# Local attention: one 128x128 score matrix for both key blocks, transposed once, spread apart before the product with the values

## The chip, the cores and the metric

The kernel runs on one core of a Trainium2 chip. The metric is the device time of one execution in microseconds. The core's engines work side by side, each through its own queue in order: TensorE (PE; its weight loads are PEld), VectorE (DVE), ScalarE (ACT), GpSimd (POOL), and SyncE (SP), whose queue issues the DMAs here.

## The reference

One decoder layer: x (4096 x 1024, float32) is projected to eight attention heads, to a gated linear attention and to gates; both branches are gated, joined, projected and normalised. The change touches the sliding-window attention alone (8 query heads of 64 in two groups that share a key and value head each, blocks of 128 rows, window 128):

```python
kb, vb = with_prev(k), with_prev(v)          # this block's 128 keys and the 128 before it
scores = einsum('bnqhgd,bnkhd->bnhgqk', qb, kb) * 64 ** -0.5
dist = qi + BLOCK - ki                       # ki from 0 to 255
in_window = (dist >= 0) & (dist < WINDOW)
scores = where(in_window & has_prev, scores, -inf)
m = maximum(scores.max(-1), sink)
p = exp(scores - m)
probs = p / (p.sum(-1) + exp(sink - m))
out = einsum('bnhgqk,bnkhd->bnqhgd', probs, vb)
```

A query q sees key k of its own block if k <= q, and key k of the block before if k > q. So for each pair (q, k) in 128 x 128 exactly one of the two scores counts.

## The kernel before, in words

The sequence is cut into 32 blocks n of 128 rows, and the work into three stages, one after the other. Stage A does the attention branch for all blocks, stage B the linear attention, stage C the output projection and the normalisation. Matrices are split in a rounded high half and the rest (`split`, L97), so a projection (`project`, L130) is three matmuls for each of eight slices of the 1024 inputs: with high weights, low weights, and low inputs (L135, L136, L137). The engines' instruction orders are made by a scheduler from the order in which the program is written and from which buffers are free; a tile pool with `bufs=1` has one buffer per tag, so a new tile waits until the last reader of the one before is done.

Stage A, the loop over n at L397, projects block n (`pq` queries, `pkv` keys and values, `pg` the gate) and weaves in the softmax and the output of block n-1, written as generators: each `next` emits the next piece between two pieces of a projection.

- `a_scores` (L286): for each group g and pair h2 of heads, four matmuls (L306) write scores of two heads against 256 keys into one PSUM bank `psc`. For each head VectorE adds the mask, scales by 0.125, writes the result `s` to SBUF and reduces the maximum (L316). Then come small 4-wide operations for a group (L329, L330), ScalarE's exponential of 128x256 with its sum (L333), small ones again (L337, L338), and GpSimd's scaling of each head by the reciprocal `rec` (L341).
- `a_out` (L345): `turn(g, b)` transposes four heads' 128x128 blocks for key block b on TensorE (L355) and splits the result in `ph` (ScalarE) and `pl` (VectorE). `mul(g, b)` multiplies both with the values `vvs` into the bank `po` (L367, L368). ScalarE and VectorE add the two halves of `po` to `att` (L371, L372).
- Four more things share the engines in each block: the rotary work and copies of `a_q` and `a_kv`, the transposes `tk` (keys) and `tq` (queries) with their splits `kd` and `qs`, the gate `sg` with its transposes `tg`, and the load of x for the block after next, cast on GpSimd to `xh` (L102) and subtracted on VectorE to `xl` (L105).

PSUM has four tags with two banks each: `pj` (projections), `tp` (transposes), `c` (scores) and `d` (`po`).

Of the kernel before, what the change touches and what calls it, by code (L numbers as in the profile page):

```python
# [19 lines left out]
P = 128  # L20
# [6 lines left out]
NEG = -3.0e38  # L27
# [23 lines left out]
def layer_kernel(  # L51
# [35 lines left out]
    def bank(tag, name):  # L87
        return ps.tile([P, 512], F32, tag=tag, name=name)
# [49 lines left out]


    with ExitStack() as pa:  # L140
        wr = pa.enter_context(tc.tile_pool(name="wra", bufs=6))
        e1 = pa.enter_context(tc.tile_pool(name="e1", bufs=1))
        e2 = pa.enter_context(tc.tile_pool(name="e2", bufs=2))
        a1 = pa.enter_context(tc.tile_pool(name="a1", bufs=1))
        a2 = pa.enter_context(tc.tile_pool(name="a2", bufs=2))
        a4 = pa.enter_context(tc.tile_pool(name="a4", bufs=4))
        a12 = pa.enter_context(tc.tile_pool(name="a12", bufs=12))

        xs = [load_x(0, act, dve)]
        wq = load_group(wr, w_a, 0, 512, 0, 512, True)  # L150
# [73 lines left out]
        def swapped(n):  # L224
            return n % 4 < (n - 1) % 4
# [59 lines left out]

        def a_scores(n, qs):  # L286

            cur, prv = n % 4, (n - 1) % 4
            lo, hi = min(cur, prv), max(cur, prv)
            mask = msk[:, (2 if n == 0 else 1) if swapped(n) else 0]  # L290
# [4 lines left out]
            rec = a2.tile([P, 8], F32, tag="rec", name=f"rec{n}")  # L295
            pn = []
            for g in range(2):
                gs = slice(4 * g, 4 * g + 4)
                sc = []
                for h2 in range(2):  # L300
                    psc = bank("c", f"psc{n}_{g}_{h2}")
                    for e in range(2):
                        h = 4 * g + 2 * h2 + e
                        o = psc[:, e * 256 : (e + 1) * 256]
                        for hl in range(2):
                            pe.matmul(  # L306
                                o,
                                qs[:, h, :],
                                kd[:, g, hl, lo : hi + 1 : hi - lo, :],
                                start=(hl == 0),  # L310
                                stop=(hl == 1),
                            )
                    for e in range(2):
                        h = 4 * g + 2 * h2 + e
                        s = a12.tile([P, 256], F32, tag="s", name=f"s{n}_{h}")
                        dve.tensor_tensor_reduce(  # L316
                            out=s,
                            in0=psc[:, e * 256 : (e + 1) * 256],
                            in1=mask,
                            scale=0.125,  # L320
                            scalar=NEG,
                            op0=ALU.add,
                            op1=ALU.max,
                            accum_out=mx[:, h : h + 1],
                        )
                        sc.append(s)
                    if h2 == 0:
                        yield
                dve.scalar_tensor_tensor(ngm[:, gs], mx[:, gs], -1.0, nsnk[:, gs], ALU.mult, ALU.min)  # L329
                dve.tensor_tensor(es[:, gs], ngm[:, gs], snk[:, gs], ALU.add)  # L330
                for i in range(4):
# [7 lines left out]
                for i in range(4):  # L339
                    h = 4 * g + i  # L340
                    pool.tensor_scalar(sc[i], sc[i], rec[:, h : h + 1], 1.0, ALU.mult, ALU.mult)  # L341
                pn.append(sc)
                yield pn

        def a_out(n, pn, sg):  # L345
# [3 lines left out]
            pos_ = [bank("d", f"po{n}_{g}") for g in range(2)]  # L349
            parts = {}  # L350

            def turn(g, b):
                pt = bank("tp", f"pt{n}_{g}_{b}")
                for i in range(4):
                    pe.transpose(  # L355
                        pt[:, i * P : (i + 1) * P], pn[g][i][:, b * P : (b + 1) * P], ident
                    )
                ph = a2.tile([P, 512], F32R, tag="ph", name=f"ph{n}_{g}_{b}")
                pl = a2.tile([P, 512], F32R, tag="pl", name=f"pl{n}_{g}_{b}")
                split(ph, pl, pt, act, dve)  # L360
                parts[g, b] = ph, pl

            def mul(g, b):
                po = pos_[g]
                ph, pl = parts.pop((g, b))
                lh = vvs[n if (b == 0) == swapped(n) else n - 1][:, g, :]
                pe.matmul(po, lh, ph, start=(b == 0), stop=False)  # L367
                pe.matmul(po, lh, pl, start=False, stop=(b == 1))  # L368
                if b == 1:
                    m, c = (slice(0, 64), slice(64, 128)) if g == 0 else (slice(64, 128), slice(0, 64))  # L370
                    act.copy(tmp[m], po[c])  # L371
                    dve.tensor_tensor(att[m], po[m], tmp[m], ALU.add)  # L372

            turn(0, 0)
            turn(0, 1)
            yield
            mul(0, 0)
            turn(1, 0)
            yield
            mul(0, 1)  # L380
            turn(1, 1)
            yield
            mul(1, 0)
            yield
            mul(1, 1)
            yield
            tg = bank("tp", f"tg{n}")
            for j in range(4):
# [8 lines left out]
        for n in range(NB):  # L397
# [460 lines left out]
```

## Time and profile before

| | |
|---|---|
| three runs, median (lowest to highest) | 1752.09 us (1750.44 to 1753.18) |
| the profiled execution | 1752.42 us, its span 1750.6 us |
| TensorE matmul busy | 1716.2 us, 98% of the span |
| VectorE, ScalarE, GpSimd busy | 1094.8, 847.9, 456.6 us |
| granted TensorE clock, mean | 0.993 |

The span is what the profiler saw of the program; the execution's own time is 1.8 us longer. A matmul's row gives its own duration, with a modelled end, and matmuls overlap: what one costs TensorE is the distance from its start to the next start. The waits of a group tell what ended the idle time ahead of its instructions. Stage A takes up roughly the first 700 us, stage B the time up to some 1280, stage C the rest.

### The profile page before, as it was taken

The page shows a single profiled execution, that of the slowest core. Times are in us where ns is not written, and L with a number is a line of the kernel's source. Part 1 is how long each engine was busy: PE and PEld are TensorE (multiplying, and loading weights), DVE is VectorE, ACT ScalarE, POOL GpSimd, SP SyncE. Part 2 cuts the span into 40 slices and gives each one's busy share as a digit, 9 for nine tenths or more (in the row PEclk, how much of TensorE's full clock was granted, in tenths as well). Part 3 has the DMA queues.
Part 4 walks back from the last instruction along what each step waited for, and adds up shares of the span by engine and source line. Part 5 has one row for each costly group of instructions (what it writes and reads, how often), then busy time and mean ns, then how long its engine had stood idle before and what let it go on. Part 6 is the DMA issues. An engine that isn't in the chain of part 4 may idle for free.

```text
span 1750.6 us, 27011 instructions
## 1 busy us (share of the span) xinstructions
PE 1716.2 (98%) x9722; PEld 1474.6 (84%) x9722; DVE 1094.8 (63%) x2802; ACT 847.9 (48%) x2128; POOL 456.6 (26%) x633
## 2 busy tenths in 40 slices
PE   7999999999999998999999999999999899999998
PEld 6788888888888887888888888888888788888886
DVE  6766666666666677566665565565556755555555
ACT  5555555455555556555555555555555622222221
POOL 3222222222222244322222222222222412222221
PEclk9999999999999999999999999999999899999999
DMA  6211111111111123111111111111111444444442
GB/s 204 91 37 37 37 37 37 43 49 37 37 37 37 37 73 105 37 37 37 38 37 37 37 37 37 37 40 41 37 37 37 156 139 145 144 145 144 145 144 84
DMA packets 65674, 120.13 MB, mean 69 GB/s; under 512 B 22658, under 2 KB 26116, under 8 KB 65540
## 3 DMA queue, kind: packets, MB, share of 16 engines
q1 hardware_dynamic: 65540, 118.41, 20.4%
q8 instruction: 76, 1.25, 0.3%
q14 instruction: 58, 0.48, 0.1%
HBM read 84.76 MB, written 33.62 MB: 68 GB/s over the span
## 4 chain that ended last, share of the span: by engine, by line
PE 57%; DVE 1%; ACT 0%; issue 0%; DMA 0%; POOL 0%; DVEq 0%; POOLq 0%; ACTq 0%
PE py L137 7%; PE py L135 7%; PE py L136 7%; PE bg L135 3%; PE bg L137 3%; PE bg L136 3%; PE bv L135 3%; PE bv L136 3%; PE bv L137 3%; PE bq L135 2%; PE bq L137 2%; PE bq L136 2%; PE bk L137 2%; PE bk L136 2%; PE bk L135 2%; PE to L679 1%
## 5 line engine op out<-in xcount | busy, mean ns | idle before, releaser
L135 PE MATMUL py<-wh,mh 128*128 128x512 f32 x512 | 200.4, 391 | 0.0
L137 PE MATMUL py<-wh,ml 128*128 128x512 f32 x512 | 200.4, 391 | 0.0
L136 PE MATMUL py<-wl,mh 128*128 128x512 f32 x512 | 200.3, 391 | 0.0
L341 POOL TENSOR_SCALAR s<-s,rec 128x256 f32<-128x256 f32 x256 | 123.8, 499 | 280.5 <-DVE ngm L329 217.3
L333 ACT ACTIVATE s<-s,ngm 128x256 f32<-128x256 f32 x256 | 127.2, 498 | 137.7 <-DVE ngm L329 132.9
L773 POOL TENSOR_TENSOR y<-y,lg 128x1024 f32<-128x1024 f32 x31 | 74.2, 2394 | 268.9 <-ACT y L772 253.5
L102 POOL TENSOR_SCALAR xh<-xraw 128x512 fp32r<-128x512 f32 x126 | 79.0, 643 | 229.2 <-PE pg L136 192.0
L316 DVE CUSTOM_DVE_ANT_0 s<-psc,msk 128x256 f32<-128x256 f32 x256 | 98.0, 420 | 31.6 <-PE psc L306 30.6
L105 DVE TENSOR_TENSOR pl<-pt,ph 128x512 fp32r<-128x512 f32 x128 | 85.7, 689 | 50.2 <-ACT ph L100 47.6
L137 PEld LDWEIGHTS py<-wh,ml 128*128 128x128 f32 x512 | 96.8, 189 | 20.0
L136 PEld LDWEIGHTS py<-wl,mh 128*128 128x128 f32 x512 | 96.8, 189 | 20.0
L135 PE MATMUL pg<-wh,xh 128*128 128x512 f32 x256 | 112.8, 440 | 0.8 <-DVE vv L249 0.8
L135 PEld LDWEIGHTS py<-wh,mh 128*128 128x128 f32 x512 | 96.8, 189 | 19.8
L100 ACT CAST ph<-pt 128x512 fp32r<-128x512 f32 x128 | 72.1, 589 | 85.0 <-PE pt L355 83.2
L527 POOL TENSOR_TENSOR qp<-bqs,ee 128x256 f32<-128x256 f32 x32 | 23.6, 738 | 337.3 <-ACT ee L524 324.0
L135 PE MATMUL pq<-wh,xh 128*128 128x512 f32 x256 | 104.9, 410 | 6.1 <-ACT wh L100 6.0
L100 ACT CAST mh<-mr 128x1024 fp32r<-128x1024 f32 x32 | 33.7, 1053 | 154.1 <-PE py L136 154.1
L135 PE MATMUL bg<-wh,xh 128*128 128x512 f32 x256 | 107.2, 419 | 0.0
L137 PE MATMUL pq<-wh,xl 128*128 128x512 f32 x256 | 103.4, 404 | 3.1 <-DVE xl L105 3.1
L135 PE MATMUL bv<-wh,xh 128*128 128x512 f32 x256 | 103.8, 405 | 0.0
L136 PE MATMUL pq<-wl,xh 128*128 128x512 f32 x256 | 103.0, 402 | 0.1
L136 PE MATMUL bv<-wl,xh 128*128 128x512 f32 x256 | 101.0, 395 | 0.0
(221 smaller groups left out, 5077.0 us busy)
## 6 DMA issues: line engine op xcount, KB each, us to landing
xraw<-in_xt_dram SPq DMA_DIRECT2D x64, 512.0 KB
mr<-mx SPq DMA_DIRECT2D x64, 256.0 KB
xr<-in_xn_dram SPq DMA_DIRECT2D x32, 512.0 KB
out_dram<-y SPq DMA_DIRECT2D x31, 512.0 KB
mx<-att SPq DMA_DIRECT2D x32, 256.0 KB
mx<-mb SPq DMA_DIRECT2D x32, 256.0 KB
wraw<-in_w_a_dram SPq DMA_DIRECT2D x16, 256.0 KB
wraw<-in_w_b_dram SPq DMA_DIRECT2D x16, 256.0 KB
```

Of the source, the lines that this page charges most:

```text
L100: act.copy(hdst, src)
L102: pool.tensor_scalar(hdst, src, 1.0, 1.0, ALU.mult, ALU.mult)
L105: leng.tensor_tensor(ldst, src, hdst, ALU.subtract)
L135: pe.matmul(dst[:, :n], a, hs[k][:, :n], start=(k == 0), stop=False)
L136: pe.matmul(dst[:, :n], a, ls[k][:, :n], start=False, stop=False)
L137: pe.matmul(dst[:, :n], b, hs[k][:, :n], start=False, stop=(k == NK - 1))
L316: dve.tensor_tensor_reduce(out=s, in0=psc[:, e * 256 : (e + 1) * 256], in1=mask, scale=0.125, scalar=NEG, op0=ALU.add, op1=ALU.max, accum_ ...
L333: act.activation(sc[i], sc[i], AF.Exp, bias=ngm[:, h : h + 1], accum_out=den[:, h : h + 1])
L341: pool.tensor_scalar(sc[i], sc[i], rec[:, h : h + 1], 1.0, ALU.mult, ALU.mult)
L527: pool.tensor_tensor(qp, B[n]["q"], ee, ALU.mult)
L679: pe.transpose(to[:, hs], og[:, hs], ident)
L773: pool.tensor_tensor(y, y, lg, ALU.mult)
```

## The change

For each pair of heads VectorE no longer adds a mask: it copies, in the PSUM bank and where k > q (`upper`), the score of the block before over the score of this block (in block 0, a very small number). What is left is one 128x128 matrix per head, of which the maximum is reduced, two heads at once. The exponential reads it from PSUM, applies the 0.125, and writes 128 columns per head into `pr`. VectorE then normalises a whole group in one operation. `turn(g)` transposes four heads once per group, ScalarE and VectorE make the high and the low half `hl`, and GpSimd spreads each half apart with two selects by position: b = 0 keeps what belongs to this block, b = 1 what belongs to the block before, with zeros elsewhere. `mul(g)` makes the four products of a group together. Scores of group 1 are written to banks of tag `d`. The pieces are woven differently into the gate's projection, and the pool for raw weights has four buffers rather than six.

```diff
-        wr = pa.enter_context(tc.tile_pool(name="wra", bufs=6))
+        wr = pa.enter_context(tc.tile_pool(name="wra", bufs=4))
...
-        msk = e1.tile([P, 3, 256], F32, tag="msk", name="msk")
-        sp.dma_start(msk.rearrange("p a b -> p (a b)"), cst[:, K_END:])
+        dve.tensor_tensor(upt, cs[:, K_CAUS : K_CAUS + P], ident, ALU.subtract)
+        upper = upt.bitcast(U32)
+        pool.memset(neg, NEG)
...
-                    psc = bank("c", f"psc{n}_{g}_{h2}")
+                    psc = bank("cd"[g], f"psc{n}_{g}_{h2}")
...
-                        dve.tensor_tensor_reduce(out=s, in0=psc[:, e * 256 : (e + 1) * 256], in1=mask, ...)
+                    v = psc.rearrange("p (e b s) -> p e b s", e=2, b=2)
+                    dve.copy_predicated(v[:, :, ci, :], upb, neg if n == 0 else v[:, :, 1 - ci, :])
+                    dve.tensor_reduce(mx[:, h : h + 2], v[:, :, ci, :], axis=AX.X, op=ALU.max)
+                    sc += [v[:, e, ci, :] for e in range(2)]
...
-                        sc[i], sc[i], AF.Exp, bias=ngm[:, h : h + 1], accum_out=den[:, h : h + 1]
+                        pr[:, i], sc[i], AF.Exp, bias=ngm[:, h : h + 1], scale=0.125, accum_out=den[:, h : h + 1]
...
-                    pool.tensor_scalar(sc[i], sc[i], rec[:, h : h + 1], 1.0, ALU.mult, ALU.mult)
+                dve.tensor_tensor(pr, pr, rec[:, gs].unsqueeze(2).to_broadcast([P, 4, P]), ALU.mult)
...
-            def turn(g, b):
+            def turn(g):
+                pt = bank("tp", f"pt{n}_{g}")
                 for i in range(4):
+                    pe.transpose(pt[:, i * P : (i + 1) * P], pn[g][:, i], ident)
+                hl = a2.tile([P, 2, 4, P], F32, tag="hl", name=f"hl{n}_{g}")
+                act.copy(hr, ptv)
+                dve.tensor_tensor(hl[:, 1].bitcast(F32R), ptv, hr, ALU.subtract)
+                for i in range(2):
+                    for b in range(2):
+                        o = a1.tile([P, 4, P], F32R, tag=f"p{b}{i}", name=f"p{b}{i}_{n}_{g}")
+                        pool.affine_select(o, hl[:, i], [[0, 4], [sg_, P]], ALU.is_gt if b else ALU.is_ge,
+                                           0.0, base=0, channel_multiplier=-sg_)
...
+            def mul(g):
+                for i in range(2):
+                    for b in range(2):
+                        pe.matmul(po, vvs[n - b][:, g, :], parts.pop((g, b, i)), ...)
...
-            project(pg, xs[n], wg, 512, 0, 2)
             next(po, None)
-            project(pg, xs[n], wg, 512, 2, 4)
+            project(pg, xs[n], wg, 512, 0, 3)
             next(po, None)
-            project(pg, xs[n], wg, 512, 4, 5)
-            next(po, None)
-            project(pg, xs[n], wg, 512, 5, 6)
+            project(pg, xs[n], wg, 512, 3, 6)
             next(po, None)
             a_turn_k(n, kks[n])
             project(pg, xs[n], wg, 512, 6, 7)
-            next(po, None)
             qs = a_turn_q(n, qks[n])
             project(pg, xs[n], wg, 512, 7, 8)
+            next(po, None)
```

TensorE's order in a middle block, from the first transposes on. Before (each row of transposes stands four times, for the four heads):

```order
L355 MATMUL pt_0_0_1196<-cs,s_0_1071 128x128
...
L355 MATMUL pt_0_1_1205<-cs,s_0_1071 128x128
...
L367 MATMUL po_0_1194<-ph_0_0_1201,vv_534 128x512
L368 MATMUL po_0_1194<-pl_0_0_1202,vv_534 128x512
L355 MATMUL pt_1_0_1222<-cs,s_4_1114 128x128
...
L367 MATMUL po_0_1194<-ph_0_1_1210,vv_893 128x512
L368 MATMUL po_0_1194<-pl_0_1_1211,vv_893 128x512
L355 MATMUL pt_1_1_1238<-cs,s_4_1114 128x128
...
L367 MATMUL po_1_1195<-ph_1_0_1227,vv_534 128x512
L368 MATMUL po_1_1195<-pl_1_0_1228,vv_534 128x512
L258 MATMUL tk_1252<-cs,kk_1180 128x128 x2
```

Now, with nine projection matmuls `pg` between the rows of `pt_0` and `pt_1`, nine between `pt_1` and the first product, and three on either side of `tq`:

```order
L351 MATMUL pt_0_1370<-cs,pr_0_1280 128x128 x4
...
L351 MATMUL pt_1_1395<-cs,pr_1_1317 128x128 x4
...
L376 MATMUL po_0_1368<-p_3_0_1378,vv_1137 128x512
L376 MATMUL po_0_1368<-p_3_0_1380,vv_864 128x512
L376 MATMUL po_0_1368<-p_3_0_1382,vv_1137 128x512
L376 MATMUL po_0_1368<-p_3_0_1384,vv_864 128x512
L260 MATMUL tk_1426<-cs,kk_1360 128x128 x2
...
L269 MATMUL tq_1434<-cs,qk_1326 128x128 x4
...
L376 MATMUL po_1_1369<-p_3_1_1403,vv_1137 128x512
```

Two groups of transposes stand where four stood, the first directly behind the keys' and values' projection, and the products of a group stand together.

GpSimd's order in the same place (the selects of group 1 of block 3, the casts of x, the first selects of block 4; the name's two digits are key block and half, then block and group):

```order
L361 AFFINE_SELECT p11_3_0_1384<-hl3_0_1375 128x512
L361 AFFINE_SELECT p00_3_1_1403<-hl3_1_1400 128x512
L361 AFFINE_SELECT p10_3_1_1405<-hl3_1_1400 128x512
L361 AFFINE_SELECT p01_3_1_1407<-hl3_1_1400 128x512
L361 AFFINE_SELECT p11_3_1_1409<-hl3_1_1400 128x512
L102 TENSOR_SCALAR xh6_1465<-xraw6_1463 128x512 x2
L361 AFFINE_SELECT p00_4_0_1603<-hl4_0_1600 128x512
```

Before, eight scalings of 128x256 stood between two pairs of casts; now eight selects of 128x512 do, and they come after the transposes rather than ahead of them.

VectorE's order now, from the first half of the output to the first scores' copy:

```order
L385 TENSOR_TENSOR att_1366<-po_0_1368,tmp_1367 64x512
L263 TENSOR_TENSOR kd<-tk_1426,kd 128x2x128
L277 TENSOR_TENSOR qs_1439<-tq_1434,qs_1439 64x512
L105 TENSOR_TENSOR xl_1466<-xraw_1463,xh_1465 128x512
L285 SCALAR_TENSOR_TENSOR sg_1460<-sg_1460,pg_1365 128x512
L279 TENSOR_TENSOR qs_1439<-tq_1434,qs_1439 64x512
L385 TENSOR_TENSOR att_1366<-po_1_1369,tmp_1367 64x512
L105 TENSOR_TENSOR xl_1466<-xraw_1463,xh_1465 128x512
L398 SCALAR_TENSOR_TENSOR att_1366<-att_1366,tg_1453 128x512
L319 COPY_PREDICATED psc_0_0_1483<-upt,psc_0_0_1483 128x2x128
```

Before, both subtractions `xl` came last in this row, directly ahead of the scores; now the first stands ahead of the gate's `sg` and the second ahead of the output's product with the gate, and all of them stand ahead of the scores.

## Rows read from the trace of the kernel before

**Rows 1.** The page: TensorE's busy time; its granted clock in 40 slices.
```profile
PE 1716.2 (98%) x9722; PEld 1474.6 (84%) x9722; DVE 1094.8 (63%) x2802; ACT 847.9 (48%) x2128; POOL 456.6 (26%) x633
...
PEclk9999999999999999999999999999999899999999
```

**Rows 2.** Windows (from:to length, busy per engine, clock, DMA share, GB/s): middle of stage A; one block.
```profile
92.00:655.00 563.00, 562.92 (x3343) 487.86 (x3342) 382.23 (x1170) 296.34 (x853) 142.07 (x276) 1.00 0.12 41
...
316.05:336.61 20.56, 20.56 (x124) 17.82 (x123) 13.92 (x44) 10.74 (x31) 4.99 (x10) 1.00 0.10 39
```

**Rows 3.** TensorE's waits, 43 to 650 us (total, times, longest); the transposes' group, whole run.
```profile
PE pt L355 <- POOL s L341: 1.7, 2, 1.5
...
L355 PE MATMUL pt<-cs,s 128*128 128x128 f32 x512 | 74.6, 276 | 6.0 <-POOL s L341 5.5
```

**Rows 4.** Timeline of TensorE around one block's transposes (start us, duration us, instruction).
```profile
316.05 1.03 PE L355 MATMUL pt<-cs,s 128*128 128x128 f32 x8
316.84 0.48 PE L135 MATMUL pg<-wh,xh 128*128 128x512 f32 x1
...
318.55 0.39 PE L368 MATMUL po<-pl,vv 128*128 128x512 f32 x1
318.78 0.60 PE L355 MATMUL pt<-cs,s 128*128 128x128 f32 x4
319.13 0.48 PE L135 MATMUL pg<-wh,xh 128*128 128x512 f32 x1
319.45 0.39 PE L136 MATMUL pg<-wl,xh 128*128 128x512 f32 x1
```

**Rows 5.** GpSimd's groups (busy us, mean ns | idle before): 92 to 655 us; a fill.
```profile
L341 POOL TENSOR_SCALAR s<-s,rec 128x256 f32<-128x256 f32 x217 | 104.0, 495 | 241.7 <-DVE ngm L329 207.9 <-DVE rec L338 32.0 <-ACT wh L100 1.8
L102 POOL TENSOR_SCALAR xh<-xraw 128x512 fp32r<-128x512 f32 x54 | 32.6, 619 | 174.1 <-PE pg L136 174.1
L105 POOL TENSOR_TENSOR wl<-wraw,wh 128x512 fp32r<-128x512 f32 x4 | 5.1, 1294 | 5.1 <-ACT wh L100 5.1
...
L469 POOL MEMSET qbl<- 128x512 f32 x2 | 1.1, 528 | 0.0
```

**Rows 6.** Groups of VectorE and ScalarE: 92 to 655 us; the last two, whole run.
```profile
L316 DVE CUSTOM_DVE_ANT_0 s<-psc,msk 128x256 f32<-128x256 f32 x216 | 82.7, 420 | 29.6 <-PE psc L306 28.7
L105 DVE TENSOR_TENSOR pl<-pt,ph 128x512 fp32r<-128x512 f32 x108 | 72.1, 689 | 39.9 <-ACT ph L100 37.4
L333 ACT ACTIVATE s<-s,ngm 128x256 f32<-128x256 f32 x216 | 107.4, 498 | 126.9 <-DVE ngm L329 122.1 <-DVE es L330 4.8
L248 ACT CAST vv<-pkv 128x128 fp32r<-128x128 f32 x28 | 7.2, 256 | 0.0
...
L585 DVE COPY_PREDICATED am<-cs,pat 128x512 f32<-128x512 uint32 x32 | 23.4, 733 | 0.1
L664 DVE TENSOR_REDUCE ms<-sq 128x4 f32<-128x512 f32 x32 | 22.0, 686 | 31.6 <-ACT sq L663 31.3
```

**Rows 7.** Timeline: a block's first scores on TensorE; VectorE taking them up.
```profile
326.32 0.63 PE L306 MATMUL psc<-kd,qs 128*128 128x256 f32 x4
...
328.97 0.43 DVE L316 CUSTOM_DVE_ANT_0 s<-psc,msk 128x256 f32<-128x256 f32 x1
```

**Rows 8.** Timeline: one small VectorE operation, GpSimd idle and busy; GpSimd's scalings, twice.
```profile
313.14 0.16 DVE L330 TENSOR_TENSOR es<-ngm,snk 128x4 f32<-128x4 f32 x1
648.60 1.22 DVE L330 TENSOR_TENSOR es<-ngm,snk 128x4 f32<-128x4 f32 x1
...
313.17 1.85 POOL L341 TENSOR_SCALAR s<-s,rec 128x256 f32<-128x256 f32 x4 [7.99 <-DVE ngm L329]
644.71 2.57 POOL L341 TENSOR_SCALAR s<-s,rec 128x256 f32<-128x256 f32 x4 [3.09 <-DVE rec L338]
```

**Rows 9.** Timeline: TensorE where stage A ends, narrow projections of stage B.
```profile
672.13 0.28 PE L135 MATMUL bq<-wh,xh 128*128 128x272 f32 x1
672.25 0.29 PE L136 MATMUL bq<-wl,xh 128*128 128x272 f32 x1
```

More of the change, by code (lines that the diff above doesn't have):

```diff
@@ L146, in layer_kernel @@
         a4 = pa.enter_context(tc.tile_pool(name="a4", bufs=4))
-        a12 = pa.enter_context(tc.tile_pool(name="a12", bufs=12))
         xs = [load_x(0, act, dve)]
@@ L289, in a_scores @@
             lo, hi = min(cur, prv), max(cur, prv)
-            mask = msk[:, (2 if n == 0 else 1) if swapped(n) else 0]
+            ci = 0 if swapped(n) else 1
             mx = a2.tile([P, 8], F32, tag="mx", name=f"mx{n}")
@@ L295, in a_scores @@
             rec = a2.tile([P, 8], F32, tag="rec", name=f"rec{n}")
+            upb = upper.unsqueeze(1).to_broadcast([P, 2, P])
             pn = []
@@ L312, in a_scores @@
                             )
[L313 to L326, printed above, removed]
+                    v = psc.rearrange("p (e b s) -> p e b s", e=2, b=2)
+                    dve.copy_predicated(v[:, :, ci, :], upb, neg if n == 0 else v[:, :, 1 - ci, :])
+                    h = 4 * g + 2 * h2
+                    dve.tensor_reduce(mx[:, h : h + 2], v[:, :, ci, :], axis=AX.X, op=ALU.max)
+                    sc += [v[:, e, ci, :] for e in range(2)]
                     if h2 == 0:
                         yield
-                dve.scalar_tensor_tensor(ngm[:, gs], mx[:, gs], -1.0, nsnk[:, gs], ALU.mult, ALU.min)
+                dve.scalar_tensor_tensor(ngm[:, gs], mx[:, gs], -0.125, nsnk[:, gs], ALU.mult, ALU.min)
                 dve.tensor_tensor(es[:, gs], ngm[:, gs], snk[:, gs], ALU.add)
+                pr = a4.tile([P, 4, P], F32, tag="pr", name=f"pr{n}_{g}")
                 for i in range(4):
@@ L338, in a_scores @@
                 dve.reciprocal(rec[:, gs], den[:, gs])
-                for i in range(4):
-                    h = 4 * g + i
-                    pool.tensor_scalar(sc[i], sc[i], rec[:, h : h + 1], 1.0, ALU.mult, ALU.mult)
-                pn.append(sc)
+                dve.tensor_tensor(pr, pr, rec[:, gs].unsqueeze(2).to_broadcast([P, 4, P]), ALU.mult)
+                pn.append(pr)
                 yield pn
@@ L363, in mul @@
-            def mul(g, b):
-                po = pos_[g]
[L365 to L372, printed above, removed]
@@ L374, in a_out @@
-            turn(0, 0)
-            turn(0, 1)
+                    pe.transpose(pt[:, i * P : (i + 1) * P], pn[g][:, i], ident)
+                hl = a2.tile([P, 2, 4, P], F32, tag="hl", name=f"hl{n}_{g}")
+                ptv = pt.rearrange("p (h s) -> p h s", h=4)
+                hr = hl[:, 0].bitcast(F32R)
+                act.copy(hr, ptv)
+                dve.tensor_tensor(hl[:, 1].bitcast(F32R), ptv, hr, ALU.subtract)
+                for i in range(2):
+                    for b in range(2):
+                        sg_ = 1 - 2 * b
+                        o = a1.tile([P, 4, P], F32R, tag=f"p{b}{i}", name=f"p{b}{i}_{n}_{g}")
+                        pool.affine_select(
+                            o,
+                            hl[:, i],
+                            [[0, 4], [sg_, P]],
+                            ALU.is_gt if b else ALU.is_ge,
+                            0.0,
+                            base=0,
+                            channel_multiplier=-sg_,
+                        )
+                        parts[g, b, i] = o
@@ new lines, in mul @@
+            def mul(g):
+                po = pos_[g]
+                for i in range(2):
+                    for b in range(2):
+                        pe.matmul(
+                            po,
+                            vvs[n - b][:, g, :],
+                            parts.pop((g, b, i)).rearrange("p h s -> p (h s)"),
+                            start=(b == 0 and i == 0),
+                            stop=(b == 1 and i == 1),
+                        )
+                m, c = (slice(0, 64), slice(64, 128)) if g == 0 else (slice(64, 128), slice(0, 64))
+                act.copy(tmp[m], po[c])
+                dve.tensor_tensor(att[m], po[m], tmp[m], ALU.add)
@@ L376, in a_out @@
+            turn(0)
             yield
-            mul(0, 0)
-            turn(1, 0)
+            turn(1)
             yield
-            mul(0, 1)
-            turn(1, 1)
+            mul(0)
             yield
-            mul(1, 0)
-            yield
-            mul(1, 1)
+            mul(1)
             yield
```

10 lines of the change are left out of this document (2 added, 8 removed).

## The prediction

> **What bounds the kernel now.** I read the page's engine totals first [rows 1]: TensorE's matmul row is busy 98% of the span at the full granted clock, and the next engine, VectorE, 63%. The busy row alone does not say that TensorE sets the pace, so I then took one stretch that holds nothing but the steady attention block [rows 2]: 563 us with TensorE never idle, GpSimd busy 142 us of it. One block, from one group of eight transposes to the next, lasts 20.56 us [rows 2, 4], and 216 score reductions in the stretch [rows 6] make 27 such blocks. TensorE waits for the softmax hardly at all there: the transposes `pt` waited 1.7 us for GpSimd between 43 and 650 us, and 5.5 us in the whole run [rows 3], the rest where stage A ends. So in the 27 blocks the time is the sum of TensorE's start-to-start distances, and whatever leaves TensorE counts, as long as no new wait replaces it.
>
> **What the change removes.** Per block TensorE loses eight of sixteen transposes. Their busy mean of 276 ns [rows 3] is not the price, since they overlap; the starts are. Eight transposes run from 316.05 to 316.84, 0.79 us, and the projection behind them takes 0.32 where a projection or product usually takes 0.23 [rows 4]: 0.79 + 0.08 = 0.87 us. Four take 0.35 + 0.08 [rows 4]; two fours are again 0.87. So 16 transposes cost 1.74, eight cost 0.87, and the block falls to 19.69 us if nothing waits. The products with the values stay eight per block, the scores sixteen.
>
> On VectorE the eight masked reductions (0.42 us each) and four subtractions `pl` [rows 6] give way to four predicated copies, four reductions, two normalisations and two subtractions. A 512-wide predicated copy took 0.73 and a 512-wide reduction 0.69 [rows 6]; the new ones are 256 wide, so I estimate 0.47 and 0.42. That is about 0.8 us more per block on an engine that is busy 13.92 of 20.56 [rows 2]: no bound by its sum. ScalarE exponentiates 128 columns a head, not 256: between a 128-wide cast's 0.26 and the old 0.50 [rows 6] I take 0.38, and it copies two halves, not four. Both engines keep spare time; their order matters, below. SP loses the 384 KB mask load; the ring for raw weights falls from six buffers to four, which only matters while weights are loaded, at both ends: I take nothing, within 2 us.
>
> **What it adds.** GpSimd loses eight scalings of 0.50 us and gets eight selects of 128x512 per block [rows 5]. The trace has no select. Nearest rows: a fill of that size 0.53 us (writes only), the cast `xh` with one input and one output 0.62, a two-input subtraction 1.29 [rows 5]. I take 0.64, since a select reads one tensor and writes one like the cast; both ends stay for the range, and above 1.29 nothing excludes it either.
>
> Is it hidden? Count from the start of the first four transposes (T = 0). The order above gives TensorE's places: second transposes at 0.44 + 9 x 0.23 = 2.53; group 0's products at 5.07, 5.30, 5.54, 5.77; then four products, two transposes, three projections, four transposes, three projections later, group 1's at 8.05 to 8.75. Group 0's high half is copied by about 1.4; its low half waits on VectorE behind the rotary work and is there at about 4.2. With a select of a us, and 0.08 for a hand-over between engines (my choice), the two low selects are usable at 4.28 + 2a and needed at 5.77: a wait of 2a - 1.49 beyond a = 0.75. Group 1 writes the same four buffers (one buffer each), so its selects start only when group 0's products have read them, about 5.54, and end four selects later: needed at 8.75, so a may be 0.78. Where group 0's selects already hold GpSimd up to 4.2 + 2a, group 1's are usable at 4.28 + 6a, and its products, pushed back by the first wait, wait another 4a - 2.98. Together, for larger a, TensorE waits 6a - 4.47 us per block. At 0.64 both are covered, the second by half a microsecond. Behind group 1's selects on GpSimd stand the two `xh` casts, and behind these, in VectorE's queue, `xl`, then the second half of the output.
>
> **The other chain** is the softmax, and it turns out nearly as long as the block. VectorE already runs late: in the trace the first scores were done at 326.95 and VectorE took them up at 328.97 [rows 7]. After the change: `att` begins at 6.9, nine operations of some 0.6 us follow, so the first scores are taken up at about 12.8. Two copies and reductions with a small operation: 14.9. Four exponentials: 16.6. Sums, reciprocal, normalising group 0: 17.8. Last copy and reduction: 19.0. Four exponentials: 20.6. Reciprocal and normalising group 1: 22.0, which is 2.3 after the next T, and TensorE wants it at 2.53. The cover is 0.2 us.
>
> That cover is touched by the select. The trace shows GpSimd and VectorE holding each other up: 4-wide operations with two SBUF inputs that take 0.16 us took 1.22 while a GpSimd subtraction ran, and four scalings took 2.57 us against 1.85 when VectorE subtracted in SBUF beside them [rows 8]. After the change the normalisation `pr` (two SBUF inputs) falls on group 0's first selects, and `xl` on the `xh` casts. On average each waits half of the operation in progress: 0.32 + 0.31 = 0.63, less cover of 0.2 to 0.3: I take a wait of 0.35 us per block. Ends: 0 (they miss each other) and 0.64 + 0.62 - 0.2 = 1.06 (a whole operation each). The Trainium skill, "GPSIMD Engine Reference", section Specifications, says that GpSimd shares its SBUF interfaces with VectorE and contends with VectorE instructions that have two SBUF inputs. The trace agrees, with 1.22 against 0.16 us, so by that rule too the change takes back part of what it gives; ignoring the rule the sum would be 9 us lower (27 x 0.35).
>
> **The sum**, against the profiled execution's 1752.42 us (span 1750.6): 27 x (0.87 - 0.35) = 14.0 saved. Five blocks at the ends of stage A save 5 x 0.87 = 4.4, but there transposes and products stand close together (at the end nine 128x272 matmuls at 0.12 us [rows 9], some 1.1 us, lie between them, while the copy, a select and their hand-overs need 2.1), so I charge 1.2 us each, 6.0; bounds 0 and 12. Net 12.4 saved: 1740.0, and as the median of the three runs is 0.3 lower, **1740 us**.
>
> **Rivals.**
> Full cover (A): no collision, ends even: 27 x 0.87 = 23.5, 1729; with the ends' 4.4 too, 1724. For it: GpSimd would be busy only 8 x 0.64 + 1.2 = 6.4 of 20 us. Against: VectorE's chain has 0.2 us of cover, and the trace shows collisions.
> Slow selects (B), the other sign: the two group-1 waits above become TensorE's. The net is nothing when 6a - 4.47 + 0.35 = 0.87, a = 0.83 us; that is the point from which it decides. At a = 1.03 the block waits 1.71 + 0.35 and the run is 27 x 1.19 + 1.6 = 34 us slower, 1786; at the two-input row's 1.29 it is 3.27 + 0.35 and 76 us slower, 1828. For it: a select makes an index, compares and chooses per element, which a cast does not, and the buffers for the four parts are single. Against: it moves no more data than the cast. The Trainium skill, "GPSIMD Engine Reference", section Performance pitfalls for Q7 kernels, gives 2.03 cycles per element for a loop that compares and selects, and 1.03 when it is unrolled twice; 512 elements at 1.2 GHz are then, as an estimate from that page, 0.87 or 0.44 us plus dispatch, one on each side of 0.83. No run here shows which.
> Late softmax (C): collisions cost the full 1.06: 27 x 0.19 + 1.6 = 7 us slower, 1759; with 0.8 it is no change, 1752. Sign: `pt` waiting for `pr` on VectorE rather than the products for GpSimd.
> The change not doing what it says would need VectorE or the products to regain the transposes; the built order shows eight fewer, so I give that nothing.
>
> **Chances.** Forecast 0.37 (1733 to 1747), A 0.17, B 0.32, C 0.14. Less than 0.2% (3.5 us) is what a measurement of this kernel can not tell from no change. C splits into 0.02 faster, 0.06 same, 0.06 slower; B gives 0.01 same, 0.31 slower. Faster 0.37 + 0.17 + 0.02 = 0.56, same 0.07, slower 0.37. The range reaches from A's 1724 to B at the two-input row, 1830; some 3 in 100 lie below, some 13 in 100 above (a select dearer than a two-input operation). The likeliest case alone: 1724 to 1748 with A.
>
> **What would show it.** Transposes x256 rather than x512, block near 20.2 us. GpSimd's select row: mean 0.6 to 0.7. TensorE's waits: few for GpSimd's selects, some for `pr` on VectorE. I am wrong by B if the products wait for the select over 0.5 us per block, by C if `pt` waits for `pr` over 0.8, by A if TensorE is again never idle. VectorE's `pr` and `xl` rows should be longer than the 0.69 of a 512-wide row [rows 6] where GpSimd runs beside them.

## The result, and the profile after

| | before | after |
|---|---|---|
| median of the runs (lowest to highest) | 1752.17 us (1750.44 to 1753.18, 4 runs) | 1724.88 us (1723.32 to 1725.71, 4 runs) |
| span of the profiled execution | 1750.6 us | 1723.3 us |

The ratio is 0.9844, 95% interval 0.9827 to 0.9861: the change takes 27.3 us off. The forecast was 12.4 off, less than half of that. The sign is right and the time is inside the outer range, but not inside the forecast's own 1733 to 1747; the rival that came nearest is A, in which hardly anything waits.

TensorE is as busy as it was [rows 1], in a shorter span. The totals of the changed kernel, from its page of the profile:

```profile
PE 1691.6 (98%) x9466; PEld 1444.3 (84%) x9466; DVE 1122.5 (65%) x2547; ACT 774.2 (45%) x2064; POOL 498.2 (29%) x634
...
PEclk9999999999999999999999999999999899999999
```

In the middle of stage A (the window's line as in [rows 2], now up to 630 us) TensorE's row has no gap either, and the transposes stand 256 times, no longer 512 [rows 3]:

```profile
92.00:630.00 538.00, 538.00 (x3098) 460.32 (x3098) 405.73 (x949) 231.95 (x795) 175.19 (x270) 1.00 0.14 44
```

```profile
L351 PE MATMUL pt<-cs,pr 128*128 128x128 f32 x256 | 38.5, 273 | 3.6 <-DVE pr L336 2.2 <-DVE den L334 1.3
```

How long a block is shows in the row that ends each block on VectorE, `att<-att,tg`, 32 of them from first to last. Before and after:

```profile
L390 DVE SCALAR_TENSOR_TENSOR att<-att,tg x32: 687/689/689, 61.7 to 704.0; 128x512 f32<-128x512 f32 x32
```

```profile
L398 DVE SCALAR_TENSOR_TENSOR att<-att,tg x32: 686/686/689, 60.0 to 676.7; 128x512 f32<-128x512 f32 x32
```

Of the 27.3 us, 1.7 are there at the first of these rows and 25.6 come between first and last (642.3 to 616.7). From TensorE's first four transposes to those of the next block a steady block lasts 19.83 us (322.27 to 342.10), where it was 20.56 [rows 2]. In the mean of 26 equal steps between `att` rows it is 19.83 (97.1 to 612.6 us) against 20.54 (99.6 to 633.8): 0.72 a block, 19.3 us in 27 blocks. The five blocks at the ends of stage A and the start ahead of them give the other 8.0.

**Where TensorE still waits.** The busy row hides it: a product's row lasts 0.39 us, the next one starts 0.23 us after it, and so one that is held back by less than the difference, 0.16, leaves no gap. The starts show it. TensorE in the block that begins at 322.27 (T):

```profile
322.27 0.60 PE L351 MATMUL pt<-cs,pr 128*128 128x128 f32 x4
...
324.79 0.60 PE L351 MATMUL pt<-cs,pr 128*128 128x128 f32 x4
...
327.31 1.27 PE L376 MATMUL po<-p,vv 128*128 128x512 f32 x4
328.42 0.38 PE L260 MATMUL tk<-cs,kk 128*128 128x128 f32 x2
...
330.47 1.08 PE L376 MATMUL po<-p,vv 128*128 128x512 f32 x4
331.39 0.60 PE L397 MATMUL tg<-cs,sg 128*128 128x128 f32 x4
```

Second transposes at T + 2.52 and first products at T + 5.04, where the working put them at 2.53 and 5.07. Group 1's four products take 0.92 us of starts (330.47 to 331.39), group 0's 1.11 (327.31 to 328.42): a wait of some 0.18 us. It falls on the fourth product, which starts 0.31 us after the third and has a row of 0.50. Its weights are `vv`, which have long been there; but the wait for its other operand, the select's output `p`, stands in the profile at the weight load. So the loads name what the wait is for, in the same stretch of stage A:

```profile
PEld po L376 <- POOL p L361: 9.0, 26, 0.4
```

9.0 us in 26 blocks are 0.35 a block on the loads, of which 0.18 reach the matmuls. So the last of group 0's selects comes a little late, in every block. The kernel before hid nothing of the kind: from 92 to 655 us its loads waited 0.5 us in all.

**The groups** of the same stretch, to be held against [rows 5, 6]:

```profile
L361 POOL TENSOR_SCALAR_AFFINE_SELECT p<-hl 128x512 fp32r<-128x512 f32 x210 | 136.2, 684 | 347.0 <-ACT hl L355 316.8 <-DVE hl L356 30.3
```

```profile
L319 DVE COPY_PREDICATED psc<-upt,psc 128x256 f32<-128x256 uint32 x108 | 45.4, 421 | 0.0
L105 DVE TENSOR_TENSOR xl<-xraw,xh 128x512 fp32r<-128x512 f32 x54 | 43.8, 812 | 1.7
...
L336 DVE TENSOR_TENSOR pr<-pr,rec 128x512 f32<-128x512 f32 x54 | 37.2, 688 | 0.9
...
L243 DVE TENSOR_TENSOR qk<-ra,rb 128x80 f32<-128x80 f32 x27 | 18.0, 668 | 0.0
L244 DVE TENSOR_TENSOR qk<-ra,rb 128x80 f32<-128x80 f32 x27 | 17.5, 649 | 0.0
```

The select's mean is 0.68 us. Three kinds of VectorE rows got longer. One is `xl`, whose mean of 0.81 mixes two: the first of each block takes 0.92 to 0.94 beside a cast, the second 0.69 alone. The others are two narrow rotary operations, 0.67 and 0.65, which before took (VectorE's groups of the kernel before, 92 to 655 us):

```profile
L241 DVE TENSOR_TENSOR qk<-ra,rb 128x80 f32<-128x80 f32 x27 | 10.9, 403 | 0.0
L242 DVE TENSOR_TENSOR qk<-ra,rb 128x80 f32<-128x80 f32 x27 | 6.3, 234 | 0.0
```

The normalisation `pr` did not: 0.69, the price of a 512-wide row. Why, the timeline of VectorE and then GpSimd in that block tells:

```profile
323.18 0.17 DVE L334 TENSOR_TENSOR den<-den,es 128x4 f32<-128x4 f32 x1 [1.47 <-ACT es L333]
...
323.87 0.69 DVE L336 TENSOR_TENSOR pr<-pr,rec 128x512 f32<-128x512 f32 x1
324.48 0.67 DVE L243 TENSOR_TENSOR qk<-ra,rb 128x80 f32<-128x80 f32 x1
325.07 0.67 DVE L244 TENSOR_TENSOR qk<-ra,rb 128x80 f32<-128x80 f32 x1
...
326.06 1.28 DVE L356 TENSOR_TENSOR hl<-pt,hl 128x512 fp32r<-128x512 f32 x2
329.29 0.68 DVE L385 TENSOR_TENSOR att<-po,tmp 64x512 f32<-64x512 f32 x1 [1.95 <-ACT tmp L384]
329.90 0.40 DVE L263 TENSOR_TENSOR kd<-tk,kd 128x256 fp32r<-128x256 f32 x1
...
331.30 0.94 DVE L105 TENSOR_TENSOR xl<-xraw,xh 128x512 fp32r<-128x512 f32 x1
...
335.64 0.42 DVE L319 COPY_PREDICATED psc<-upt,psc 128x256 f32<-128x256 uint32 x1
```

```profile
324.03 1.03 POOL L361 TENSOR_SCALAR_AFFINE_SELECT p<-hl 128x512 fp32r<-128x512 f32 x1 [12.16 <-ACT hl L355]
...
326.81 3.57 POOL L361 TENSOR_SCALAR_AFFINE_SELECT p<-hl 128x512 fp32r<-128x512 f32 x6 [1.17 <-DVE hl L356]
330.49 1.21 POOL L102 TENSOR_SCALAR xh<-xraw 128x512 fp32r<-128x512 f32 x2
```

`pr` began at 323.87, the first select 0.16 us later, and it is the select whose row is long: 1.03 instead of 0.63. GpSimd had the time. The next select runs until about 325.6, and beside it the two rotary operations are the long ones. Behind them on VectorE stands group 0's low half `hl` (T + 3.79), and for that the low selects wait: they start at 326.81, six in 3.57 us, 0.60 each, so the last one of group 0 starts at 327.41 and, with a row of 0.63, ends at 328.04. The fourth product had its place at 327.31 + 3 x 0.23 = 328.00; its load starts at 328.08.

### The profile page after: what moved, and what is told of

It reads as the page before. It is cut to its first block, busy times and chain, and to the rows that moved or that the text cites. A ratio compares the mean times of both kernels' runs of the same rounds, so it can differ in the third digit from the quotient of the medians.

```text
span 1723.3 us, 26109 instructions
## 1 busy us (share of the span) xinstructions
PE 1691.6 (98%) x9466; PEld 1444.3 (84%) x9466; DVE 1122.5 (65%) x2547; ACT 774.2 (45%) x2064; POOL 498.2 (29%) x634
## 4 chain that ended last, share of the span: by engine, by line
PE 58%; DVE 1%; ACT 1%; issue 0%; DMA 0%; POOL 0%; DVEq 0%; POOLq 0%; ACTq 0%
PE py L135 7%; PE py L137 7%; PE py L136 7%; PE bg L135 3%; PE bg L137 3%; PE bg L136 3%; PE bv L135 3%; PE bv L136 3%; PE bv L137 3%; PE bq L135 2%; PE bq L136 2%; PE bq L137 2%; PE bk L137 2%; PE bk L136 2%; PE bk L135 2%; PE to L684 1%
## 5 line engine op out<-in xcount | busy, mean ns | idle before, releaser
L361 POOL TENSOR_SCALAR_AFFINE_SELECT p<-hl 128x512 fp32r<-128x512 f32 x256 | 165.6, 682 | 382.7 <-ACT hl L355 348.8
L330 ACT ACTIVATE pr<-psc,ngm 128x128 f32<-128x128 f32 x256 | 90.7, 367 | 193.8 <-PE psc L311 138.1
L100 ACT CAST mh<-mr 128x1024 fp32r<-128x1024 f32 x32 | 33.7, 1054 | 154.2 <-PE py L136 154.2
L105 DVE TENSOR_TENSOR xl<-xraw,xh 128x512 fp32r<-128x512 f32 x128 | 94.7, 760 | 11.6 <-ACT xh L100 5.2
L136 PE MATMUL pg<-wl,xh 128*128 128x512 f32 x256 | 100.6, 393 | 1.3 <-POOL wl L105 1.0
L137 PE MATMUL pg<-wh,xl 128*128 128x512 f32 x256 | 101.0, 395 | 0.0
L137 PE MATMUL bg<-wh,xl 128*128 128x512 f32 x256 | 100.7, 393 | 0.0
```

Source lines behind the costliest of these rows:

```text
L100: act.copy(hdst, src)
L105: leng.tensor_tensor(ldst, src, hdst, ALU.subtract)
L136: pe.matmul(dst[:, :n], a, ls[k][:, :n], start=False, stop=False)
L137: pe.matmul(dst[:, :n], b, hs[k][:, :n], start=False, stop=(k == NK - 1))
L330: act.activation(pr[:, i], sc[i], AF.Exp, bias=ngm[:, h : h + 1], scale=0.125, accum_out=den[:, h : h + 1])
L361: pool.affine_select(o, hl[:, i], [[0, 4], [sg_, P]], ALU.is_gt if b else ALU.is_ge, 0.0, base=0, channel_multiplier=-sg_,)
```

## The experiments

**One: is it the transposes?** On the changed kernel, each group of transposes issued twice.

```diff
-                for i in range(4):
-                    pe.transpose(pt[:, i * P : (i + 1) * P], pn[g][:, i], ident)
+                for r in range(2):
+                    for i in range(4):
+                        pe.transpose(pt[:, i * P : (i + 1) * P], pn[g][:, i], ident)
```

> The changed kernel with each of its eight transposes per block issued twice, the second time over the same bank. Theory 1 (the gain is TensorE's shorter queue: what leaves it counts by its distance from start to start): eight more starts at 0.089 us are 0.71 us per block, 23 us over 32 blocks; the 0.14 us that the products still wait in a block may go, since they come later by as much, so 19 to 23 us over the changed kernel's 1724.9: 1744 to 1748. Theory 2 (the transposes were hidden and the gain came from the softmax, the masks or the ends): under 5 us more, below 1730.

Measured: 1746.18 us, ratio to before 0.9967 (0.9956 to 0.9979). Eight more transposes a block cost 21.3 us over the changed kernel, in 32 blocks 0.67 each. That is as expected, and most of the gain. It is less than their price, because the wait for the selects goes: from 92 to 630 us no matmul and no weight load waits, and the steady block is 20.50 us (311.06 to 331.56), 0.85 above a block without waits (19.65, below).

**Two: the other way round.** The kernel before with only the first key block's transposes and splits, used for both key blocks. It leaves out the probabilities of the second key block.

```diff
             turn(0, 0)
-            turn(0, 1)
             yield
+            parts[0, 1] = parts[0, 0]
             mul(0, 0)
             turn(1, 0)
             yield
             mul(0, 1)
-            turn(1, 1)
+            parts[1, 1] = parts[1, 0]
```

> The kernel before with only the first half of each group's transposes and their splits; the products use that half for both key blocks, so the second key block's probabilities are left out of the output. Masks, softmax, scalings, banks and buffers stay as before. Theory 1: 0.87 us per block less on TensorE and nothing new to wait for: 32 x 0.87 = 28 us faster, 1724, so this one part gives the whole gain. Theory 2: the ends' 7.6 us come from the banks, the mask load or the order at the start, so that only 27 x 0.87 = 23 us or less appear: 1729 to 1740.

Measured: 1727.57 us, ratio 0.9857 (0.9840 to 0.9875). Leaving out eight transposes a block, and four of the eight splitting operations, takes 24.6 us off a kernel that has none of the new work: 0.77 a block. The time lies between those of the two theories. Here a new wait takes something back, for the low half:

```profile
PEld po L368 <- DVE pl L105: 7.2, 26, 0.3
```

So both runs, 21 and 25 us, put the transposes a little low.

**Three: how far are the selects from deciding?** On the changed kernel, each select issued twice.

```diff
-                        pool.affine_select(
+                        for r in range(2):
+                            pool.affine_select(
```

> The changed kernel with each select issued twice, the second writing the same again, so that a select costs GpSimd 1.2 us and not 0.6. Theory 1 with the places read from its trace: the low selects of group 0 end some 1.2 us after they are needed, those of group 1 some 1.9 us after, 3.1 us a block against 0.14 now: 27 x 2.95 = 80 us slower, about 1805 (my forecast's formula, 6a - 4.47 at 1.2, gives 2.73 a block and 1795). Rival: only GpSimd's sum counts, 11 us of a block of 20, so no change, 1725.

Measured: 1819.02 us, ratio 1.0375 (1.0353 to 1.0397). TensorE's weight loads, 92 to 630 us, against 9.0 us with single selects:

```profile
PEld po L377 <- POOL p L362: 84.3, 96, 1.5
```

Its steady block, from transposes at 316.52 to the next at 339.35, is 22.83 us: 3.2 more than a block without waits (19.65, below). The formula 6a - 4.47 gives 2.7 for a = 2 x 0.60. So rival B was a real mechanism, at somewhat more than the working's price; the run is 14 us above the expectation. It did not happen because the select costs 0.60 from start to start, and not 0.83.

**Four: does the new weave matter?** The changed kernel with the pieces at their old places in the gate's projection.

```diff
+            project(pg, xs[n], wg, 512, 0, 2)
             next(po, None)
-            project(pg, xs[n], wg, 512, 0, 3)
+            project(pg, xs[n], wg, 512, 2, 4)
             next(po, None)
-            project(pg, xs[n], wg, 512, 3, 6)
+            project(pg, xs[n], wg, 512, 4, 5)
+            next(po, None)
+            project(pg, xs[n], wg, 512, 5, 6)
             next(po, None)
...
-            next(po, None)
```

> The changed kernel with its pieces at the old places in the gate's projection: transposes after two and four of eight slices, the products after five and six. Theory 1: only three projections lie between the second transposes and the first products, and three between the products, so the selects are late by some 0.6 and 0.7 us: 1.3 us a block against 0.14, 27 x 1.16 = 31 us slower, about 1756. Rival: the selects are hidden wherever the pieces stand: no change, 1725.

Measured: 1751.6 us, ratio 1.0001 (0.9991 to 1.001). The whole gain is gone although the transposes stay at eight; the run is 4 us below the expectation. Its waits, weight loads from 92 to 630 us:

```profile
PEld po L376 <- POOL p L361: 35.6, 103, 0.4
PEld tg L397 <- DVE kd L263: 6.2, 26, 0.2
```

Four products a block wait for their select, where one does now. With the selects between them and the products, fewer transposes are worth something only because the products were moved away.

**Five and six: what is the wait that is left?** Five moves group 0's products behind the keys' transposes. Six casts x on ScalarE, not GpSimd.

```diff
-            next(po, None)
             a_turn_k(n, kks[n])
+            next(po, None)
```

> The changed kernel with group 0's products placed behind the two transposes of the keys, 0.2 us later in TensorE's order. Theory 1: the 0.14 us that they wait in a block for the low selects is covered, and nothing else moves: up to 27 x 0.14 = 4 us faster, 1721 to 1725. Rival: the wait moves on to group 1's products, whose selects start later by as much: no change.

```diff
-                xs.append(load_x(n + 1, pool, dve))
+                xs.append(load_x(n + 1, act, dve))
```

> The changed kernel with the cast of x on ScalarE rather than GpSimd, so that VectorE's two subtractions xl no longer meet a GpSimd cast. Theory 1: this collision (0.94 against 0.69 us in a block) is off the path that sets the time: no change, 1725 within 2 us. Theory of my forecast (collisions cost TensorE 0.35 us a block, half of it through xl): up to 5 us faster, 1720.

Measured: five 1720.61 us, ratio 0.9818 (0.9804 to 0.9831); six 1718.44 us, ratio 0.9808 (0.9794 to 0.9821). Five comes out at the fast end of what was expected: its block is 19.70 us, and 4.7 us of waits for the selects are left on its loads. Six contradicts the reading that the casts, which run ten microseconds before the next transposes, are off the path: it saves 6.4 us on the changed kernel, a little more than the forecast's theory gave. VectorE in a block of six that begins at T = 319.79:

```profile
320.45 0.16 DVE L334 TENSOR_TENSOR den<-den,es 128x4 f32<-128x4 f32 x1 [1.47 <-ACT es L333]
...
323.32 1.28 DVE L356 TENSOR_TENSOR hl<-pt,hl 128x512 fp32r<-128x512 f32 x2
...
328.65 0.69 DVE L105 TENSOR_TENSOR xl<-xraw,xh 128x512 fp32r<-128x512 f32 x1
...
332.75 0.42 DVE L319 COPY_PREDICATED psc<-upt,psc 128x256 f32<-128x256 uint32 x1
```

`xl` is back at 0.69, the first scores are taken up at T + 12.96 (changed kernel 13.37), `den` of group 1 comes at T + 0.66 (0.91) and the low half at T + 3.53 (3.79). Its steady block is 19.66 us (319.79 to 339.45) and group 0's products take the normal 0.94. The rotary rows are as long as they were. So by these rows the cast reaches the products by a whole turn of the block: `xl`, first scores, softmax, low half, last select.

**Seven and eight: the ends.** Seven is the kernel before with its score banks spread over two tags, as the change has them. Eight is the changed kernel with six raw buffers again.

```diff
-                    psc = bank("c", f"psc{n}_{g}_{h2}")
+                    psc = bank("cd"[g], f"psc{n}_{g}_{h2}")
```

> The kernel before with the scores of group 1 in the banks of the output, as in the changed kernel, and nothing else changed. If the ends' 7.6 us came from the banks: 1 to 4 us faster than before, 1748 to 1751, and the wait of the scores for VectorE's reduction (1.2 us, once) gone. If they came from the transposes: no change, 1752.

```diff
-        wr = pa.enter_context(tc.tile_pool(name="wra", bufs=4))
+        wr = pa.enter_context(tc.tile_pool(name="wra", bufs=6))
```

> The changed kernel with six buffers for raw weights as before, not four. Expected under both theories: no change within 2 us; if the smaller ring had cost time at the ends, up to 2 us faster, and if it had helped by changing the order at the start, up to 3 us slower, with TensorE's wait for xl back at 3 us.

Measured: seven 1750.3 us, ratio 0.9988 (0.9980 to 0.9997), about 2 us; eight 1725.23 us, ratio 0.9847 (0.9834 to 0.9860), no difference to the changed kernel, although TensorE's wait for `xl` at the start is back at 3.0 us.

**Nine to eleven: one chain or several costs?** Nine joins five and six. Ten moves the rotary work behind the first transposes, so that it stands behind group 0's low half on VectorE. Eleven is ten with six. The core of ten:

```diff
-                kks[m] = a_kv(m, pkv, qks[m])
...
             next(po, None)
+            for m in group:
+                kks[m] = a_kv(m, pkvs[m], qks[m])
```

> The two edits that each took some microseconds off the changed kernel, together: the cast of the x tiles on ScalarE and the keys' transposes ahead of group 0's products. Theory: both remove the same wait, the 0.14 us a block of group 0's products for the selects, and with either of them alone the block already stands at 19.66 to 19.68 us, TensorE's own work; together they give no more than the better one, 1717 to 1719 us. Rival: they act on separate costs and add (4.3 + 6.4 us): 1714 us.

> The rotary work of the block's keys and queries moved on VectorE behind the first transposes of the probabilities, so that group 0's low half stands right behind the scaling of group 1. Theory: group 0's products wait 0.14 us a block because the low half starts 3.79 us after the transposes, behind two narrow rotary operations that the selects stretch from 0.40 and 0.23 to 0.67 and 0.65 us; ahead of them it starts at about 2.4, the four selects are done before the products' place, and the block is 19.7 us: 1720 to 1722 us. Rival: only the take-up of the first scores counts (13.37 us after the transposes, which this leaves): no change, 1724 to 1726. If the keys come too late for their own transposes in return, slower than 1726.

> The same with the cast of the x tiles on ScalarE. Theory: nothing is left to wait in a steady block, so it equals the cast on ScalarE alone, 1717 to 1719 us. Rival: the gains add, 1714.

Measured: nine 1720.64 us (0.9819, 0.9806 to 0.9833), ten 1719.74 (0.9816, 0.9802 to 0.9829), eleven 1721.0 (0.9821, 0.9808 to 0.9834). The gains don't add: five, six and nine to eleven stand within 2.6 us of each other, with intervals that overlap. Ten is as expected. Nine and eleven come out 1.6 and 2 us above what they were to reach at most, within those intervals. VectorE in a block of ten with T = 320.76:

```profile
322.37 0.69 DVE L336 TENSOR_TENSOR pr<-pr,rec 128x512 f32<-128x512 f32 x1
322.97 0.68 DVE L356 TENSOR_TENSOR hl<-pt,hl 128x512 fp32r<-128x512 f32 x1
323.57 0.65 DVE L243 TENSOR_TENSOR qk<-ra,rb 128x80 f32<-128x80 f32 x1
324.15 0.67 DVE L244 TENSOR_TENSOR qk<-ra,rb 128x80 f32<-128x80 f32 x1
```

The low half starts at T + 2.21. The rotary operations are stretched as before, but nothing that TensorE wants soon stands behind them, and the block is 19.64 us (320.76 to 340.40). At the end of stage A ten pays back some of it: there TensorE waits 2.5 us for `vv`, which `a_kv` now makes later, and from 627.7 us, 0.9 us after that wait, its granted clock is at half, 1.2 GHz, for 3.4 us:

```profile
PE pg L135 <- DVE vv L251: 2.5, 1, 2.5
```

So the remaining wait is one chain. Breaking it takes 0.13 us off a block in five, 0.17 in six and 0.18 in ten (19.70, 19.66 and 19.65 in the mean), and two edits together, nine and eleven, leave the block at 19.67 and 19.66. No wait for another engine stands on the weight loads of the steady blocks of six, nine, ten and eleven, so what is left is TensorE's own work. The fastest of these kernels by its median is six, 33.7 us under the kernel before.

## Why the prediction was wrong, and where it was right

The gain was more than twice the forecast. The parts that the change takes away were priced right; two charges set against them were too high: the collisions in the steady block, and new waits at the ends.

**Transposes removed: right.** 0.87 a block was forecast. A block without waits is 19.64 to 19.66 us (ten, six), so 0.9 went.

**The select: right.** 0.64 was taken and rows of 0.63 to 0.64 are its usual length; the mean is 0.68 for the one in eight that starts beside `pr`. What counts for the queue, from start to start, is 0.60. That decided against rival B; doubling the select showed that B's mechanism was there, at 22.83 us a block. Of the two estimates that the prediction worked out from the Trainium skill's "GPSIMD Engine Reference", section Performance pitfalls for Q7 kernels, the measured 0.60 excludes 0.87; 0.44 would leave 0.16 for the dispatch, which the prediction gave no figure for and no run here measures.

**The softmax chain: right in its end, wrong in one place.** `pr` of group 1 was to be ready at 2.3 after T; it ended at 324.56, T + 2.29. That is partly luck, two errors that cancel: the first scores were taken up at 13.37, not 12.8 (`xl` stretched ahead of them), and shorter steps behind them, exponentials spaced 0.35 rather than 0.38 among them, made that good. On VectorE the working said about 0.8 us more per block; its own prices add up to 0.2 (6.32 against 6.12), and the busy time grew by 1.0 (14.95 against 13.95). That sum bounds nothing; the order of the operations does.

**The step that failed first: "on average each waits half of the operation in progress: 0.32 + 0.31", 0.35 a block.** It put the collision on `pr`, and had TensorE's transposes wait for it. Measured: 0.18 a block, and on the products; the transposes waited for no other engine. Collisions are there, but the one at `pr` fell on the select, which began after it and had time; the one at the casts was 0.25 on the first `xl` of a block, near the 0.31; and a third, not foreseen, on two narrow rotary operations (0.40 and 0.23 to 0.67 and 0.65) delayed the low half. The low half was to be there at 4.2 and was at 326.06 + 0.6 to 0.7, T + 4.4 to 4.5, which used up the 0.21 us of cover that the working gave the low selects (1.49 - 2 x 0.64). The Trainium skill, "GPSIMD Engine Reference", section Specifications, says that GpSimd contends with VectorE instructions that have two SBUF inputs. The rows of the changed kernel agree: VectorE's stretched rows are all of that kind, while `att` and `kd`, which read one input from PSUM, began inside selects and stayed at 0.68 and 0.40. Experiment ten has a stretched row that is not of that kind, a copy with one input: `kk`, 0.28 in the changed kernel, where GpSimd is idle then, and here, beside a select:

```profile
324.94 0.52 DVE L246 COPY kk<-qk 128x256 f32<-128x256 f32 x1
```

Which of the two engines pays has to be read from the starts. In the steady blocks this step is worth 27 x (0.35 - 0.18) = 4.6 us of the error; transposes at 0.9 rather than 0.87 give some 0.7 more.

**The step that failed worse: "I charge 1.2 us each, 6.0".** The five end blocks were to lose 1.6 us net; the ends gained 8.0, which makes 9.6 of the 15 us of error. TensorE's waits in the kernel before, from 40 to 78 us (beside the 1.7 us for `s` of [rows 3], which lie there) and from 632 to 735:

```profile
PE psc L306 <- DVE mx L316: 1.2, 1, 1.2
```

```profile
PE pt L355 <- POOL s L341: 3.8, 3, 2.9
PE po L368 <- DVE pl L105: 1.6, 1, 1.6
PE pat L583 <- DVE qbl L568: 1.3, 1, 1.3
```

In the changed kernel, 40 to 74 and 609 to 707 us:

```profile
PE pt L351 <- DVE den L334: 1.3, 1, 1.3
PE pg L136 <- POOL wl L105: 0.6, 1, 0.6
PE pt L351 <- DVE pr L336: 0.4, 1, 0.4
```

```profile
PE po L376 <- POOL p L361: 1.9, 4, 1.0
PE pt L351 <- DVE pr L336: 1.8, 1, 1.8
PE pat L588 <- DVE qbl L573: 1.4, 1, 1.4
PE psc L311 <- DVE qs L279: 0.7, 1, 0.7
```

Products do wait for selects there, as the prediction said, but 1.9 us in all. And the charge set no credit against it. The kernel before already waited at these places for its own softmax and splits (`s`, `pl`, `mx`), 8.3 us by these rows. The changed one waits 6.7 (`den`, `wl`, `pr` twice, `p`, `qs`); the wait in stage B, `pat`, is the same in both. That is 1.6 us less where 6.0 more were charged. With 5 x 0.9 for transposes it makes 6.1 of the 8.0. Another 1.3 us lie further ahead: the first `pkv` projection starts at 24.78, not at 26.12. Experiment eight does not settle what the raw buffers do there: with six, TensorE waits 3.0 us for `xl` again and `pkv` starts at 25.44, but the total time stays. A mask load that is gone and the order of the first splits were not tried apart. The spread of the score banks is worth 2 us by experiment seven (0.5 to 3.5 by its interval), where the wait for `mx` is gone and one of 0.7 us for `qs` stands in its place.

How the 8.0 divide is not shown any closer, because TensorE's clock is mixed into them. The working took it at full; in the steady stretch it was, but in the profile of the kernel before it was granted at half, 1.2 GHz, in two stretches of the ends (columns as in [rows 2]):

```profile
14.90:21.70 6.80, 5.97 (x14) 4.71 (x15) 5.25 (x13) 4.05 (x10) 1.34 (x3) 0.50 0.51 154
677.10:680.50 3.40, 3.02 (x14) 2.70 (x15) 1.16 (x4) 1.54 (x4) 3.40 (x7) 0.50 0.45 154
```

The first fell inside the 3.1 us that TensorE waited for `xl`; the `pq` projections stand 0.43 us apart in it, and 0.23 behind it. In the changed kernel the waits there are 1.1 and 1.2 us, and `pq` is at 0.23 from 18.4 us, not from 21.8: of the 1.3 us ahead of `pkv` some 0.9 are of this kind, the rest shorter waits. The second fell 0.5 us after TensorE had waited 2.9 us for `s`; narrow projections `bq` stand 0.23 us apart in it rather than 0.12, and by such distances it costs up to 1.4 us, as an estimate. In the changed kernel TensorE waits 1.8 us for `pr` at that place and the clock stays at 2.4 GHz. Clock and time also differ between executions of one kernel: the kernel before took 1749.1 to 1750.2 us where its mean granted clock was 0.996 or 0.997, and 1752.3 to 1754.3 where it was 0.992 or 0.993. So a part of the ends' gain is the clock's, by these numbers an estimated 1 to 2 us.

That A's 1724 is the measured time to a microsecond is therefore luck: A had no collision, and the ends at 4.4; measured were 0.18 us of wait in each block, and 8.0 at the ends.

**The weave: counted without a price of its own.** The prediction took the new places as given. Experiment four shows that at the old places the products' waits eat the full gain.

## What to carry to other kernels

Where one engine is always busy, taking work from it pays in full only if each thing it reads is made with cover, so move the consumer away from the producer in the same edit, and check the cover by doubling the producer. When you charge a new wait at the ends of a stage, first list what the old kernel waits for at the same places, and charge the difference. A wait of some tenths can hang on a chain that runs once around the whole block: several edits that each remove it don't add.

## What had not been expected of the hardware

In the block shown, where a VectorE instruction with two SBUF inputs overlapped with one of GpSimd, the one that started later was the long one: select 1.03 us beside `pr`, `pr` itself 0.69. It can hit small work hardest: a 128x80 operation of 0.23 us took 0.65 beside a select, while the 512-wide `xl`, 0.69 alone, took 0.92 to 0.94 beside a cast. The 0.23 was itself taken beside GpSimd's scalings, of 0.5 us each.

A matmul that is held back by a tenth of a microsecond shows no idle time. Over 538 us TensorE's row was full, and yet 0.18 us a block were lost; the longer row (1.27 for four products, not 1.08) and the waits of the weight loads showed it, though the operand that came late was not the weights.
